# A hybrid decoder step: the sampled tokens' caches go through load, GpSimd product and VectorE sum in three staggered steps, and their HGRN states are loaded one item ahead

## The chip, the cores and the metric

One core of one Trainium2 chip runs the whole program. The metric is the device time of one execution in microseconds, taken as the median of several runs. Five instruction streams matter: PE (TensorE, matmuls), DVE (VectorE), ACT (ScalarE), POOL (GpSimd) and SP (SyncE, which issues every DMA of this kernel). Each stream is worked off in order, and an instruction that waits for a semaphore holds up everything behind it on its own stream.

## The reference

One layer of a decoder trunk, all in float32, for a prompt of 2048 tokens and 8 sampled tokens (one new token for each of 8 sequences with caches). Cut to what matters here:

```python
u = rmsnorm(h) @ w_in                       # 1024 -> 10752 columns, prompt and sampled tokens together
# A: dilated window attention, 3 groups x 8 heads x 64;  B: HGRN2, 4 heads, state 128x128
# C: cross-attention, 4 heads x 128, 256 memory tokens;  then three sigmoid merge gates
# sampled tokens:
s = einsum('bshd,bsjhd->bshj', q, cached_k) * Dh**-0.5       # A: 129 keys, each sequence its own cache
o = einsum('bshj,bsjhd->bshd', softmax(s), cached_v)
S_new = f * S_old + k outer v;  o = S_new^T q                # B: 8 sequences x 4 heads of 128x128
sc = einsum('bthd,bmhd->bhtm', q, mem_k);  oc = einsum('bhtm,bmhd->bthd', softmax(sc), mem_v)   # C
merged = sig(ga) * (ya @ w_pa) + sig(gb) * (yb @ w_pb) + sig(gc) * (yc @ w_pc)
out = h + rmsnorm(merged @ w_out)
```

Every sequence has its own keys and values, so the sampled tokens' products are elementwise work and not matmuls: GpSimd multiplies a block of 128x512 numbers, VectorE sums it.

## The kernel before

The input projection is 36 *units* of 256 columns over five chunks of tokens (512, 384, 384, 384 and 392 wide). Every product is three matmuls (L402, L403, L404), since each operand is split into a rounded part and a rest. The last 24 units are a Python generator, `gate_stream`; beside it run other generators: prompt attention, prompt HGRN, and in the last phase (`phase_rest`) the prompt's cross-attention (`cross`) and `sample`, the sampled tokens' four parts one after the other: `sample_heads`, `sample_attention`, `sample_hgrn`, `sample_cross`. A loop hands out turns: a generator yields (cost, gap), the cost being its matmul time in that step and the gap how long it wants to be left alone before its next turn. While no other generator is due, the next 24 or so matmuls of `gate_stream` are written. So the gaps set only one thing directly: the order of the matmuls on PE, which is kept exactly as written (`manual_schedule(engines={PE})`). On the other engines a scheduler places the instructions when the program is built, by dependences and by its own estimate of times.

After the loop comes the branch stage: matmuls at L163 to L165 (`mm3`), with weights loaded at L1214 and split at L1215 and L1216, inputs loaded at L1226 and split at L1227 and L1229, products with the gates at L1250.

What the change touches:

- Cache blocks. A block of keys or values is 128x512 numbers (256 KB). It lands in one of three slots of the ring `skv`, GpSimd multiplies it in place (L1000 keys, L1027 values, L1094 memory keys, L1121 memory values), VectorE sums it (L1001; L1029 and L1030; L1095; L1123 and L1124). There are 20, 20, 16 and 16 blocks. Between keys and values stands a softmax over all blocks' scores. At the end of each part one small matmul gathers the result (L1036 for the window caches, L1128 for the memory).
- HGRN items. Eight items (4 heads x 2 halves of the batch). Each loads a state of 256 KB into one of two buffers (`ss0`, L1058) and the values, repeated over 128 partitions, into a slot of `skv` (L1061); GpSimd multiplies (L1062), VectorE scales the state and adds (L1063, L1064), the new state is stored (L1065), and after a gap of 2 us four tiny matmuls read it (L1069).
- `cross` writes its score matmuls at L898, its maxima at L899, its normalisation on VectorE at L907, the transposes on PE at L918 that need L907, and the value matmuls at L929. Every gate chunk leaves PSUM through L494 on VectorE. There are three PSUM banks for the gate stream.

Of the kernel before, what the change touches and what calls it, by code (L numbers as in the profile page):

```python
# [10 lines left out]
F32 = mybir.dt.float32  # L11
F32R = mybir.dt.float32r
AF = mybir.ActivationFunctionType
ALU = mybir.AluOpType
# [83 lines left out]
def tile_hybrid_step(ctx: ExitStack, tc: tile.TileContext, I: dict, O: dict):  # L98
# [854 lines left out]
    def sample_heads(sps, pool):  # L953

        cols = pool.tile([128, 28, DEC], F32, tag="scols", name="s_cols", bufs=1)
        dma(cols[:, 0:12, :], qT[:, :, SEQ:NT].rearrange("j p b -> p j b"))
        dma(cols[:, 12:24, :], kT[:, :, SEQ:NT].rearrange("j p b -> p j b"))
        dma(cols[:, 24:28, :], cqT[:, :, SEQ:NT].rearrange("j p b -> p j b"))
        yield 0.0, 5.0
        for i in range(7):  # L960
            ps = sps.tile([128, 512], F32, tag="sp", name="s_pr")
            for j in range(4):
                T.transpose(ps[:DEC, j * 128:j * 128 + 128], cols[:, i * 4 + j, :], ident)
            row = pool.tile([128, 512], F32, tag="skv", name="s_row", bufs=3)[:DEC, :]
# [17 lines left out]

    def sample_attention(sps, pool):
# [5 lines left out]
        for g in range(3):  # L989
# [7 lines left out]
            for j0 in range(0, nj[g], 8):  # L997
                kc = pool.tile([128, 8, 64], F32, tag="skv", name="s_kc", bufs=3)
                dma(kc, I[f"kc{g}"][:, j0:j0 + 8, :])
                G.tensor_tensor(kc, kc, q.unsqueeze(1).to_broadcast([128, 8, 64]), op=ALU.mult)  # L1000
                V.tensor_reduce(sc[:, base[g] + j0:base[g] + j0 + 8], kc, axis=AX.X, op=ALU.add)  # L1001
                yield 0.0, SA_GAP
# [19 lines left out]
        for g in range(3):  # L1022
            for j0 in range(0, nj[g], 8):
                vc = pool.tile([128, 8, 64], F32, tag="skv", name="s_vc", bufs=3)
                dma(vc, I[f"vc{g}"][:, j0:j0 + 8, :])
                pj = sc[:, base[g] + j0:base[g] + j0 + 8]
                G.tensor_tensor(vc, vc, pj.unsqueeze(2).to_broadcast([128, 8, 64]), op=ALU.mult)  # L1027
                t = pool.tile([128, 64], F32, tag="st64", name="s_t", bufs=1)
                V.tensor_reduce(t, vc.rearrange("p j d -> p d j"), axis=AX.X, op=ALU.add)  # L1029
                V.tensor_tensor(o, o, t, op=ALU.add)  # L1030
                yield 0.0, SA_GAP
# [12 lines left out]
    def sample_hgrn(sps, pool):  # L1044
# [8 lines left out]
        for h in range(4):  # L1053
            hgrn_gates(pool, e[:, h, :], lb[:, h:h + 1], oml[:, h:h + 1], f[:, h, :], kin[:, h, :], DEC)
            for b0 in (0, 4):
                bs = slice(b0, b0 + 4)
                s0 = pool.tile([128, 4, 128], F32, tag="ss0", name="s_s0")
                dma(s0, I["state"][:, h, bs, :])  # L1058
                vb = pool.tile([128, 4, 128], F32, tag="skv", name="s_vb", bufs=3)
                sh = [128, 4, 128]  # L1060
                dma(vb, vS[bs, 1536 + h * 128:1664 + h * 128].unsqueeze(0).to_broadcast(sh))  # L1061
                G.tensor_tensor(vb, vb, kin[:, h, bs].unsqueeze(2).to_broadcast(sh), op=ALU.mult)  # L1062
                V.tensor_tensor(s0, s0, f[:, h, bs].unsqueeze(2).to_broadcast(sh), op=ALU.mult)  # L1063
                V.tensor_tensor(s0, s0, vb, op=ALU.add)  # L1064
                dma(O["hg_s"][bs, h].rearrange("b k v -> k b v"), s0)  # L1065
                yield 0.0, SA_GAP
                for b in range(4):
                    c = h * DEC + b0 + b
                    T.matmul(po[:, c:c + 1], lhsT=s0[:, b, :], rhs=q[:, h, b0 + b:b0 + b + 1], start=True, stop=True)  # L1069
                yield 1.65, 0.0  # L1070
# [15 lines left out]
    def sample_cross(sps, pool):  # L1086
# [4 lines left out]
        for j in range(16):  # L1091
            kc = pool.tile([128, 4, 128], F32, tag="skv", name="s_xk", bufs=3)
            dma(kc, I["mkc"][:, j * 4:j * 4 + 4, :])
            G.tensor_tensor(kc, kc, q.unsqueeze(1).to_broadcast([128, 4, 128]), op=ALU.mult)  # L1094
            V.tensor_reduce(s[:, j * 4:j * 4 + 4], kc, axis=AX.X, op=ALU.add)  # L1095
            yield 0.0, SA_GAP
# [21 lines left out]
        for j in range(16):  # L1118
            vc = pool.tile([128, 4, 128], F32, tag="skv", name="s_xv", bufs=3)
            dma(vc, I["mvc"][:, j * 4:j * 4 + 4, :])  # L1120
            G.tensor_tensor(vc, vc, s[:, j * 4:j * 4 + 4].unsqueeze(2).to_broadcast([128, 4, 128]), op=ALU.mult)  # L1121
# [3 lines left out]
            yield 0.0, SA_GAP  # L1125
# [299 lines left out]
```

## Time and profile before

| | |
|---|---|
| median of 3 runs | 3144.35 us (3142.03 to 3147.8) |
| the profiled execution | 3151.64 us, span 3149.9 us |
| PE / LDWEIGHTS / VectorE / ScalarE / GpSimd busy | 96% / 87% / 45% / 32% / 32% |
| first to last small transposes of `sample_heads` (L963) | from 2319.5 us to 2337.8 us |
| matmul after the window caches (L1036) | 2535.3 us |
| HGRN matmuls (L1069) | 2539.7 to 2583.9 us |
| matmul after the memory caches (L1128) | 2675.2 us |

PE is the long engine, so what matters are the places where it stands still. In the rows of the profile, times in brackets are the idle time of the engine just before an instruction and what ended it. A matmul's duration overlaps the next matmul's; the pace is the distance of two starts. PEclk is the share of the TensorE clock that was granted.

### The profile page before, as it was taken

To read this page: it belongs to the slowest core of one execution; us is meant where nothing else is said; L and a number is where in the kernel's file an instruction comes from. 1 tells how busy PE (TensorE), PEld (TensorE's weight loads), DVE (VectorE), ACT (ScalarE), POOL (GpSimd) and SP (SyncE) were. 2 spreads that over 40 slices of the span, in tenths; PEclk is the share of its full clock that TensorE was granted. 3 is DMA by queue.
4 is the path that set the end of the run, shared out by engine and by line. 5 is a ranking of instruction groups with operands and counts; after the bars stand their busy time and mean duration, and the time that the engine had idled before them with its cause. 6 is when DMAs were issued, how large, how long until landed. Compare 5 with 4: busy or idle time off the path is not lost. (4 is left out here: it accounts for less than half of the span.)

```text
span 3149.9 us, 56777 instructions
## 1 busy us (share of the span) xinstructions
PE 3017.3 (96%) x22028; PEld 2746.6 (87%) x22028; DVE 1402.9 (45%) x3635; ACT 995.7 (32%) x2468; POOL 1020.5 (32%) x836
## 2 busy tenths in 40 slices
PE   6999999999999999999899999999998988999998
PEld 6999999999999887878788888888886877899986
DVE  8700002222223555465652376777757356233232
ACT  4412110000003654444551344444443433201222
POOL 4312126556654112020222331121125125634411
PEclk9999999999999999999999999999999999999999
DMA  4333222122213457475645322232246466666442
GB/s 138 102 99 88 72 74 81 61 74 77 71 68 108 120 144 196 136 199 140 175 126 161 98 87 93 88 103 92 90 129 181 116 167 213 199 180 178 155 147 95
DMA packets 369311, 387.54 MB, mean 123 GB/s; under 512 B 87881, under 2 KB 292297, under 8 KB 365713
## 3 DMA queue, kind: packets, MB, share of 16 engines
q1 hardware_dynamic: 369040, 383.91, 41.2%
q8 instruction: 173, 2.83, 0.4%
q14 instruction: 98, 0.79, 0.1%
HBM read 245.13 MB, written 138.67 MB: 122 GB/s over the span
## 5 line engine op out<-in xcount | busy, mean ns | idle before, releaser
L402 PE MATMUL bank<-rnd 128*128 128x384 f32 (+2 forms) x2880 | 1041.4, 362 | 14.7 <-DVE side L494 8.4
L404 PE MATMUL bank<-rnd 128*128 128x384 f32 (+2 forms) x2880 | 1009.1, 350 | 4.6 <-POOL rnd L201 4.6
L403 PE MATMUL bank<-rnd 128*128 128x384 f32 (+2 forms) x2880 | 1009.2, 350 | 0.0
L402 PEld LDWEIGHTS bank<-rnd 128*128 128x128 f32 x2880 | 548.7, 191 | 55.0 <-DVE side L494 9.4
L404 PEld LDWEIGHTS bank<-rnd 128*128 128x128 f32 x2880 | 547.8, 190 | 30.2 <-POOL rnd L201 5.5
L403 PEld LDWEIGHTS bank<-rnd 128*128 128x128 f32 x2880 | 548.8, 191 | 23.1 <-issue 1.9
L163 PE MATMUL bank<-rnd 128*128 128x256 f32 (+4 forms) x1648 | 531.4, 322 | 8.6 <-DVE raw L1250 4.9
L165 PE MATMUL bank<-rnd 128*128 128x256 f32 (+4 forms) x1648 | 528.4, 321 | 4.3 <-POOL rnd L248 4.3
L164 PE MATMUL bank<-rnd 128*128 128x256 f32 (+4 forms) x1648 | 528.7, 321 | 0.6 <-DVE rnd L1229 0.6
L201 POOL TENSOR_TENSOR rnd<-raw,rnd 128x512 fp32r<-128x512 f32 x172 | 227.7, 1331 | 610.7 <-ACT rnd L200 609.3
L163 PEld LDWEIGHTS bank<-rnd 128*128 128x128 f32 (+1 forms) x1648 | 312.6, 190 | 25.1 <-issue 4.2
L165 PEld LDWEIGHTS bank<-rnd 128*128 128x128 f32 (+1 forms) x1648 | 312.6, 190 | 17.8 <-POOL rnd L248 5.3
L164 PEld LDWEIGHTS bank<-rnd 128*128 128x128 f32 (+1 forms) x1648 | 312.7, 190 | 13.8 <-DVE rnd L1229 1.3
L200 ACT CAST rnd<-raw 128x512 fp32r<-128x512 f32 x172 | 106.1, 619 | 631.8 <-PE bank L403 453.8
L450 DVE TENSOR_TENSOR raw<-bank,raw 128x384 f32<-128x384 f32 (+2 forms) x120 | 70.4, 587 | 444.2 <-POOL side L455 214.6
L583 ACT ACTIVATE raw<-raw 128x256 f32<-128x256 f32 (+1 forms) x384 | 172.9, 452 | 152.4 <-DVE raw L581 152.3
L491 POOL TENSOR_TENSOR side<-side 128x384 f32<-128x384 f32 (+2 forms) x60 | 65.6, 1093 | 260.2 <-ACT side L490 242.3
L495 ACT ACTIVATE side<-side 128x384 f32<-128x384 f32 (+2 forms) x120 | 65.5, 546 | 242.7 <-DVE side L494 236.6
L1250 DVE TENSOR_TENSOR raw<-raw,bank 128x412 f32<-128x412 f32 (+1 forms) x120 | 66.9, 579 | 166.4 <-DMA raw<-sgT 87.1
L696 POOL TENSOR_TENSOR side<-side 128x512 f32<-128x512 f32 x32 | 51.1, 1596 | 241.0 <-DMA side<-stC 74.9
L1254 POOL TENSOR_TENSOR raw<-raw 128x412 f32<-128x412 f32 (+1 forms) x80 | 89.8, 1123 | 96.2 <-DVE raw L1250 90.1
L598 ACT COPY raw<-bank 128x256 f32<-128x256 f32 (+1 forms) x192 | 87.2, 492 | 101.1 <-PE bank L596 99.3
(265 smaller groups left out, 3896.5 us busy)
## 6 DMA issues: line engine op xcount, KB each, us to landing
raw<-in_w_t SPq DMA_DIRECT2D x144, 256.0 KB
raw<-sgT SPq DMA_DIRECT2D x96, 206.0 KB
sgT<-side SPq DMA_DIRECT2D x72, 192.0 KB
qT<-side SPq DMA_DIRECT2D x12, 1028.0 KB
out_kT<-side SPq DMA_DIRECT2D x12, 1028.0 KB
out_vN<-raw SPq DMA_DIRECT2D x96, 128.0 KB
raw<-qT SPq DMA_DIRECT2D x96, 128.0 KB
raw<-out_kT SPq DMA_DIRECT2D x96, 128.0 KB
```

Source lines behind the costliest of these rows:

```text
L163: T.matmul(out, lhsT=lh, rhs=rh, start=(i == 0), stop=False)
L164: T.matmul(out, lhsT=lh, rhs=rl, start=False, stop=False)
L165: T.matmul(out, lhsT=ll, rhs=rh, start=False, stop=(i == n - 1))
L200: A.copy(hi, raw)
L201: G.tensor_tensor(lo, raw, hi.bitcast(F32), op=ALU.subtract)
L402: T.matmul(ps[:, :w], lhsT=hi, rhs=xh[c][:, k, :], start=(k == 0), stop=False)
L403: T.matmul(ps[:, :w], lhsT=hi, rhs=xl[c][:, k, :], start=False, stop=False)
L404: T.matmul(ps[:, :w], lhsT=lo, rhs=xh[c][:, k, :], start=False, stop=(k == KT - 1))
L450: V.tensor_tensor(t1[:, :w], ps[:, :w], rc[:, c0:c0 + w], op=ALU.mult)
L583: A.activation(sm[:, :w], sm[:, :w], AF.Exp, scale=-1.0, bias=nmc, accum_out=sts[hp][:, g, 1, h, idx:idx + 1])
L598: A.copy(pts[:, :, :nb, :], pt[:, :, :nb, :])
L1254: G.tensor_tensor(acc[:, :w], acc[:, :w], gt[:, :w], op=ALU.add)
```

## The change

The ring `skv` has four slots in place of three. Key and value blocks of all four passes go through a new generator `in_turn`: in step i block i is loaded, block i-1 is multiplied, block i-2 is summed, and each step yields a gap of 2 us, so each pass has two steps more than it has blocks. In `sample_hgrn` the loads of item i are written ahead of the work on item i-1; the gaps of an item are 2.5 us after the loads and 4.0 us between the new state and its matmuls, where there was 2.0 us.

```diff
+    def in_turn(pool, srcs, first, second):
+        n, tiles = len(srcs), {}
+        for i in range(n + 2):
+            if i < n:
+                tiles[i] = pool.tile([128] + list(srcs[i].shape[1:]), F32, tag="skv", name="s_c", bufs=4)
+                dma(tiles[i], srcs[i])
+            if 0 < i <= n:
+                first(i - 1, tiles[i - 1])
+            if i > 1:
+                second(i - 2, tiles.pop(i - 2))
+            yield 0.0, SA_GAP
...
-            for j0 in range(0, nj[g], 8):
-                kc = pool.tile([128, 8, 64], F32, tag="skv", name="s_kc", bufs=3)
-                dma(kc, I[f"kc{g}"][:, j0:j0 + 8, :])
+            def multiply(i, kc):
                 G.tensor_tensor(kc, kc, q.unsqueeze(1).to_broadcast([128, 8, 64]), op=ALU.mult)
-                V.tensor_reduce(sc[:, base[g] + j0:base[g] + j0 + 8], kc, axis=AX.X, op=ALU.add)
-                yield 0.0, SA_GAP
+            def reduce(i, kc):
+                V.tensor_reduce(sc[:, base[g] + 8 * i:base[g] + 8 * i + 8], kc, axis=AX.X, op=ALU.add)
+            yield from in_turn(pool, [I[f"kc{g}"][:, j0:j0 + 8, :] for j0 in range(0, nj[g], 8)], multiply, reduce)
...
-        for h in range(4):
-            hgrn_gates(...)
-            for b0 in (0, 4):
-                s0 = ...; dma(s0, I["state"][:, h, bs, :])
-                vb = ...; dma(vb, vS[...])
+        for i in range(len(items) + 1):
+            if i < len(items):
+                h, b0 = items[i]
+                s0 = pool.tile(sh, F32, tag="ss0", name="s_s0")
+                dma(s0, I["state"][:, h, b0:b0 + 4, :])
+                vb = pool.tile(sh, F32, tag="skv", name="s_vb", bufs=4)
+                dma(vb, vS[...])
+                states[i] = s0, vb
+                yield 0.0, 2.5
+            if i == 0:
+                continue
+            h, b0 = items[i - 1]
+            s0, vb = states.pop(i - 1)
+            if b0 == 0:
+                hgrn_gates(...)
                 G.tensor_tensor(vb, vb, kin...); V.tensor_tensor(s0, s0, f...); V.tensor_tensor(s0, s0, vb, op=ALU.add)
                 dma(O["hg_s"][bs, h].rearrange("b k v -> k b v"), s0)
-                yield 0.0, SA_GAP
+            yield 0.0, 4.0
                 # 4 matmuls (128x1); yield 1.65, 0.0
```

The window values, the memory keys and the memory values get the same edit as the window keys, with `weigh` and `add` for the values. In the rows below, lines of the changed kernel are: L989 every cache load, L1074 a state's load, L1076 the values' load, L1086 GpSimd's product for an HGRN item, L1089 the state's store, L1093 its matmuls, L1098 the HGRN norm's matmul, L1039 the window values' product, L1116 and L1119 product and sum of memory keys, L1144, L1148 and L1149 those of memory values, L1154 the matmul after the memory caches, L1240 and L1242 load and split of branch weights, L1252 and L1255 those of branch inputs, L1276 the product with the gates (L1250 before).

PE, at the end of the gate stream, before: one matmul of the sampled tokens stands between the last gate matmul (L404) and the branch stage (L163).

```order
L404 MATMUL bank_96<-rnd 128x392
L1128 MATMUL bank_103<-c_sel_c,f_15660 128x32
L163 MATMUL bank_98<-rnd 128x412
L164 MATMUL bank_98<-rnd 128x412
L165 MATMUL bank_98<-rnd 128x412
```

The same place now.

```order
L404 MATMUL bank_96<-rnd 128x392
L1093 MATMUL bank_103<-f_15660 128x1 x4
L1098 MATMUL bank_103<-f_15660,ones_v 128x32
L1154 MATMUL bank_103<-c_sel_c,f_15660 128x32
L163 MATMUL bank_98<-rnd 128x412
```

What moved: the eighth HGRN item's matmuls and the HGRN norm have come down to the end of the gate stream. In all, the first L1069 stood 487 rows ahead of L163 and the eighth 386; the first L1093 stands 277 rows ahead and the eighth 3.

POOL, from the window values to the branch stage, before.

```order
L1027 TENSOR_TENSOR side<-side 128x512 x11
L1062 TENSOR_TENSOR side<-side 128x512 x5
L201 TENSOR_TENSOR rnd<-raw,rnd 128x512 x8
L1062 TENSOR_TENSOR side<-side 128x512 x3
L1094 TENSOR_TENSOR side<-side,f_15660 128x512 x16
L1121 TENSOR_TENSOR side<-side,f_15660 128x512 x3
L201 TENSOR_TENSOR rnd<-raw,rnd 128x512 x2
L1121 TENSOR_TENSOR side<-side,f_15660 128x512 x8
L1229 TENSOR_TENSOR rnd<-raw,rnd 128x824
```

And now (L201 splits the last weights of the gate stream).

```order
L1039 TENSOR_TENSOR side<-side 128x512 x20
L1086 TENSOR_TENSOR side<-side,f_15660 128x512 x6
L201 TENSOR_TENSOR rnd<-raw,rnd 128x512 x10
L1086 TENSOR_TENSOR side<-side,f_15660 128x512
L1255 TENSOR_TENSOR rnd<-raw,rnd 128x824
L1242 TENSOR_TENSOR rnd<-raw,rnd 128x512
L1086 TENSOR_TENSOR side<-side,f_15660 128x512
L1242 TENSOR_TENSOR rnd<-raw,rnd 128x512 x2
L1255 TENSOR_TENSOR rnd<-raw,rnd 128x824
L1116 TENSOR_TENSOR side<-side,f_15660 128x512
L1255 TENSOR_TENSOR rnd<-raw,rnd 128x824
L1116 TENSOR_TENSOR side<-side,f_15660 128x512
```

What moved: 19 of the 32 products of the memory caches stood ahead of the split of the gate stream's last two weight pieces; now none does, and they stand among the branch stage's splits.

SP, around the state loads of the sixth to the eighth item, before (L498 stores one chunk of a gate, so that two of them are a chunk apart).

```order
L1058 DMA f_15660<-in_state 128x512
L498 DMA sgT<-side 128x384
L1065 DMA out_hg_s<-f_15660 128x4x128
L1061 DMA side<-out_vS 128x4x128
L1065 DMA out_hg_s<-f_15660 128x4x128
L931 DMA yT<-raw 128x512
L1058 DMA f_15660<-in_state 128x512
L1093 DMA side<-in_mkc 128x512
L926 DMA raw<-szT 128x512
L1058 DMA f_15660<-in_state 128x512
```

And now, from the seventh state's load; each of these state loads waits on a semaphore of PE.

```order
L1074 DMA f_15660<-in_state 128x512
L498 DMA sgT<-side 128x384
L989 DMA side<-in_mkc 128x512 x2
L1240 DMA raw<-in_w_br 128x4x128 x2
L498 DMA sgT<-side 128x384
L1089 DMA out_hg_s<-f_15660 128x4x128
L989 DMA side<-in_mkc 128x512 x3
L1074 DMA f_15660<-in_state 128x512
```

What moved: behind the eighth state's load 18 chunks of gates were still to be stored, and one memory block stood ahead of it; now four chunks are left behind it, and seven memory blocks stand ahead.

More of the change, by code (lines that the diff above doesn't have):

```diff
@@ L1022, in sample_attention, with weigh, add @@
         for g in range(3):
[L1023 to L1026, printed above, removed]
+            def weigh(i, vc):
+                pj = sc[:, base[g] + 8 * i:base[g] + 8 * i + 8]
                 G.tensor_tensor(vc, vc, pj.unsqueeze(2).to_broadcast([128, 8, 64]), op=ALU.mult)
+            def add(i, vc):
                 t = pool.tile([128, 64], F32, tag="st64", name="s_t", bufs=1)
@@ L1030, in sample_attention @@
                 V.tensor_tensor(o, o, t, op=ALU.add)
-                yield 0.0, SA_GAP
+            yield from in_turn(pool, [I[f"vc{g}"][:, j0:j0 + 8, :] for j0 in range(0, nj[g], 8)], weigh, add)
             e = base[g] + nj[g]
@@ L1052, in sample_hgrn @@
         po, pn = bank[:, 0:32], bank[:, 32:64]
-        for h in range(4):
-            hgrn_gates(pool, e[:, h, :], lb[:, h:h + 1], oml[:, h:h + 1], f[:, h, :], kin[:, h, :], DEC)
-            for b0 in (0, 4):
[L1056 to L1070, printed above, removed]
+        sh = [128, 4, 128]
@@ new lines, in sample_hgrn @@
+        items, states = [(h, b0) for h in range(4) for b0 in (0, 4)], {}
+        for i in range(len(items) + 1):
[4 more added lines that the diff above has]
+                vb = pool.tile(sh, F32, tag="skv", name="s_vb", bufs=4)
+                dma(vb, vS[b0:b0 + 4, 1536 + h * 128:1664 + h * 128].unsqueeze(0).to_broadcast(sh))
+                states[i] = s0, vb
[3 more added lines that the diff above has]
+            h, b0 = items[i - 1]
+            bs = slice(b0, b0 + 4)
+            s0, vb = states.pop(i - 1)
+            if b0 == 0:
+                hgrn_gates(pool, e[:, h, :], lb[:, h:h + 1], oml[:, h:h + 1], f[:, h, :], kin[:, h, :], DEC)
+            G.tensor_tensor(vb, vb, kin[:, h, bs].unsqueeze(2).to_broadcast(sh), op=ALU.mult)
+            V.tensor_tensor(s0, s0, f[:, h, bs].unsqueeze(2).to_broadcast(sh), op=ALU.mult)
+            V.tensor_tensor(s0, s0, vb, op=ALU.add)
+            dma(O["hg_s"][bs, h].rearrange("b k v -> k b v"), s0)
+            yield 0.0, 4.0
+            for b in range(4):
+                c = h * DEC + b0 + b
+                T.matmul(po[:, c:c + 1], lhsT=s0[:, b, :], rhs=q[:, h, b0 + b:b0 + b + 1], start=True, stop=True)
+            yield 1.65, 0.0
@@ L1090, in sample_cross, with multiply, reduce @@
         s = pool.tile([128, 64], F32, tag="sxs", name="s_xs", bufs=1)
-        for j in range(16):
-            kc = pool.tile([128, 4, 128], F32, tag="skv", name="s_xk", bufs=3)
-            dma(kc, I["mkc"][:, j * 4:j * 4 + 4, :])
+        def multiply(i, kc):
             G.tensor_tensor(kc, kc, q.unsqueeze(1).to_broadcast([128, 4, 128]), op=ALU.mult)
-            V.tensor_reduce(s[:, j * 4:j * 4 + 4], kc, axis=AX.X, op=ALU.add)
-            yield 0.0, SA_GAP
+        def reduce(i, kc):
+            V.tensor_reduce(s[:, 4 * i:4 * i + 4], kc, axis=AX.X, op=ALU.add)
+        yield from in_turn(pool, [I["mkc"][:, j * 4:j * 4 + 4, :] for j in range(16)], multiply, reduce)
         m = pool.tile([128, 4], F32, tag="sxm", name="s_xm", bufs=1)
@@ L1117, in sample_cross, with weigh, add @@
         V.memset(o, 0.0)
[L1118 to L1121, printed above, removed]
+        def weigh(i, vc):
+            G.tensor_tensor(vc, vc, s[:, 4 * i:4 * i + 4].unsqueeze(2).to_broadcast([128, 4, 128]), op=ALU.mult)
+        def add(i, vc):
             t = pool.tile([128, 128], F32, tag="sxt", name="s_xt", bufs=1)
@@ L1124, in sample_cross @@
             V.tensor_tensor(o, o, t, op=ALU.add)
-            yield 0.0, SA_GAP
+        yield from in_turn(pool, [I["mvc"][:, j * 4:j * 4 + 4, :] for j in range(16)], weigh, add)
         yield 0.0, SA_LAG
```

2 lines of the change are left out of this document (1 added, 1 removed).

## The prediction, made before the changed kernel ran

> **What bounds the kernel now.** I read the page first, then the busy times by stretch, the PE timeline where it stands still, and the timelines of the engines that it waits for.
>
> ```profile
> span 3149.9 us, 56777 instructions
> PE 3017.3 (96%) x22028; PEld 2746.6 (87%) x22028; DVE 1402.9 (45%) x3635; ACT 995.7 (32%) x2468; POOL 1020.5 (32%) x836
> ```
>
> PE is busy for all but 133 us. A change that touches no matmul can win only where PE stands still and lose only where it makes PE stand. The table by stretch says where the sampled tokens' work costs anything (columns: stretch, its length, busy us of PE, its weight loads, VectorE, ScalarE, GpSimd, granted clock, DMA share, GB/s).
>
> ```profile
> 2319.60:2535.30 215.70, 191.57 (x966) 167.19 (x963) 121.38 (x279) 90.88 (x231) 68.59 (x61) 0.95 0.53 146
> 2390.00:2430.00 40.00, 32.41 (x158) 27.69 (x157) 37.49 (x80) 16.67 (x46) 22.01 (x24) 0.96 0.68 203
> 2450.00:2535.00 85.00, 85.00 (x437) 74.91 (x436) 31.20 (x80) 41.53 (x104) 12.10 (x10) 0.99 0.41 116
> 2535.30:2675.00 139.70, 118.35 (x610) 107.30 (x610) 82.00 (x162) 50.86 (x111) 60.39 (x48) 0.95 0.70 201
> 2675.00:2745.00 70.00, 62.72 (x323) 60.99 (x322) 18.81 (x31) 19.19 (x31) 46.04 (x36) 0.98 0.63 186
> ```
>
> From the first small transposes to the matmul behind the window caches PE idles 24.1 us, from there to the end of the gate stream (2675 us) 21.4 us, at the start of the branch stage 7.3 us. The stretch 2450 to 2535, where only prompt work and gates run, has none. So at most 53 us of idle time are to be had, and the slow clock behind each stop:
>
> ```profile
> 2373.78 1.08 PE L918 MATMUL bank<-ident,raw 128*128 128x128 f32 x4 [3.84 <-DVE raw L907]
> 2447.55 1.11 PE L918 MATMUL bank<-ident,raw 128*128 128x128 f32 x4 [10.72 <-DVE raw L907]
> 2564.70 1.11 PE L918 MATMUL bank<-ident,raw 128*128 128x128 f32 x4 [5.59 <-DVE raw L907]
> 2643.66 0.45 PE L402 MATMUL bank<-rnd 128*128 128x384 f32 x1 [2.37 <-DVE side L494]
> 2647.78 0.34 PE L404 MATMUL bank<-rnd 128*128 128x384 f32 x1
> 2652.36 0.44 PE L402 MATMUL bank<-rnd 128*128 128x384 f32 x1 [4.24 <-DVE side L494]
> 2655.37 0.52 PE L403 MATMUL bank<-rnd 128*128 128x384 f32 x1
> 2655.69 0.52 PE L404 MATMUL bank<-rnd 128*128 128x384 f32 x1
> ```
>
> The 24 matmuls of a chunk take 4.1 us from the first start (2643.66) to the last (2647.78), 0.18 us each. After the stop of 4.24 us the starts are 0.32 us apart for about 3 us, which loses some 1.5 us. With two to four such stops in each of the first two stretches I put them at 29 us each, idle and slow clock together.
>
> Who holds PE up is the cross-attention's normalisation (L907) or a gate's evacuation (L494) on VectorE, and these stand in VectorE's queue behind sums that wait for GpSimd, which waits for a load:
>
> ```profile
> 2431.53 0.23 DVE L1030 TENSOR_TENSOR side<-side 128x64 f32<-128x64 f32 x1
> 2437.95 0.69 DVE L1064 TENSOR_TENSOR f<-f,side 128x512 f32<-128x512 f32 x1 [6.19 <-POOL side L1062]
> 2445.09 0.69 DVE L1064 TENSOR_TENSOR f<-f,side 128x512 f32<-128x512 f32 x1 [5.65 <-POOL side L1062]
> 2429.73 14.14 DMA side<-out_vS
> ```
>
> The last row is from the chain of waits: one load of an HGRN item's values took 14.14 us.
>
> No load, product, sum or store is added or removed in any part; all of the change is order and a slot more.
>
> **Part 1: the window caches.** The edit writes the sum two steps behind the load, but only PE keeps the written order, and on VectorE the sums stand among the same gate evacuations as before, about four to a chunk. What really changes there is the fourth slot. In the key pass a slot's cycle sets the pace:
>
> ```profile
> L1000 POOL TENSOR_TENSOR side<-side x20: 1273/1295/1311, 2339.3 to 2384.5; 128x512 f32<-128x512 f32 x20
> 2339.30:2387.00 47.70, 41.88 (x196) 35.74 (x195) 30.84 (x58) 19.42 (x47) 30.30 (x24) 0.93 0.62 187
> ```
>
> 19 steps in 45.2 us are 2.38 us a block, 7.1 us a slot. Four slots give 1.8 us, 34 us for the pass, above the 1.3 us that GpSimd needs. PE idles 5.8 us in the pass (47.7 less 41.9), some 8 with the slow clock; that should mostly go, I take 7. In the value pass VectorE is busy 37.5 of 40 us (stretch 2390 to 2430), so a slot more brings nothing there: 0. For the two waits behind L1064, the values' loads still come one behind the other (the waits of 6.19 and 5.65 us are for consecutive ones) and are issued one block earlier: 2 of the 10.7 us go. Together 9 us gained; bounds -3 (four such loads in flight together slow the first) and 20.
>
> **Part 2: from there to the gates' end.** The tiny matmuls' gaps add up to 52 us (8 x 6.5) where they were 16, and the passes have 16 steps more (two for each of eight runs of blocks). On PE the first L1093 now stands 277 rows ahead of L163, at about 0.2 us a row 55 us, and the last one behind the gates. So between the window caches and that point PE sees only what the clean stretch 2450 to 2535 shows. Then come the HGRN items, one each 8 us of matmuls. The load of item i waits until PE has read item i-2, 16 us ahead of its own matmuls. A load takes
>
> ```profile
> 2551.05 11.62 DMA f<-in_state
> 2569.44 6.63 DMA f<-in_state
> ```
>
> so with 1.4 us on VectorE (0.69 each above) it is in time for items 3 to 7. The wait for PE is one on SP: behind each state's load stand a gate chunk's store, memory blocks and branch weights. Three banks and two output buffers give a gate chunk about two chunks, 8 us, before PE feels a late store, so I cost this at nothing; if loads took 16 us, PE would stop at each item. The memory sums, which made VectorE late at 2643 and 2652, have left this stretch nearly all. What stays are the branch inputs' splits on VectorE. I take 22 of the 29 us as gained; bounds 10 and 29.
>
> **Part 3: the memory caches, behind the gates.** Here the change costs. Before, the last memory sum was done 17 us ahead of the gates' end, and the matmul behind it cost nothing:
>
> ```profile
> L1128 PE MATMUL bank<-c_sel_c,f x2: 190/232/273, 2675.2 to 2675.2; 128*128 128x32 f32 x2
> 2658.03 0.59 DVE L1124 TENSOR_TENSOR f<-f 128x128 f32<-128x128 f32 x1
> ```
>
> Now L1154 still stands ahead of every branch matmul, and the memory blocks must take the slots of HGRN values that are freed only by the sums of items 5 to 8. PE then waits with nothing else to do. I follow the slot of item 8, with 0 at the end of the gate matmuls.
>
> - Item 8's state waits for PE's item 6, some 63 gate matmuls x 0.18 = 11 us ahead of 0, and stands on SP behind memory blocks whose slots are not yet free: issued at -7. With 6.6 us of loading and 1.4 of VectorE, the slot is free at +1 (-5 to +6).
> - Memory keys 4, 8, 12 and 16 pass through this slot one after the other. Pace before:
>
> ```profile
> L1094 POOL TENSOR_TENSOR side<-side,f x16: 1262/1291/1415, 2576.7 to 2610.1; 128x512 f32<-128x512 f32 x16
> 2618.46 3.04 POOL L1121 TENSOR_TENSOR side<-side,f 128x512 f32<-128x512 f32 x3 [7.04 <-DVE f L1115]
> L1121 POOL TENSOR_TENSOR side<-side,f x16: 1037/1042/1812, 2618.5 to 2654.7; 128x512 f32<-128x512 f32 x16
> L1123 DVE TENSOR_REDUCE f<-side x16: 1028/1080/1123, 2619.5 to 2656.6; 128x128 f32<-128x512 f32 x16
> L1124 DVE TENSOR_TENSOR f<-f x16: 276/407/1758, 2621.0 to 2658.0; 128x128 f32<-128x128 f32 x16
> L1216 POOL TENSOR_TENSOR rnd<-raw,rnd 128x512 fp32r<-128x512 f32 x24 | 31.6, 1327 | 28.3 <-ACT rnd L1215 22.2 <-DMA raw<-in_w_br 6.2
> ```
>
> 15 steps in 33.4 us, 2.23 us a block, 6.7 us a slot's cycle: 4 x 6.7 = 27, to +28 (22 to 32 for the term).
> - The softmax between the passes left GpSimd 7.0 us without work: +35 (6 to 7).
> - 16 value blocks took 15 steps of 2.41 us; a slot's cycle of 7.2 us over four slots is 1.8 us, 29 us (24 to 38). GpSimd's own work in it is no less than 16 x 1.04 and, by POOL's order, about seven branch-weight splits of 1.3: 26 us. With 2 us for the last sums: L1154 at +66.
>
> The VectorE addition L1124 took from 0.28 to 1.76 us for the same shape. The Trainium skill, page "SBUF — State Buffer", section "SBUF: two separate sides", says that VectorE and GpSimd hold one pair of ports exclusively for a whole instruction when VectorE reads two SBUF tensors. The spread here looks like that, though these rows alone don't prove it. By that rule the additions and GpSimd's products exclude each other, 16 x (1.04 + 0.28) + 7 x 1.3 = 30 us in place of 29, and the tail would be 67 us; it speaks against a gain from the fourth slot in this pass.
>
> **Part 4: the branch stage.** Its weights and first inputs are split while PE waits, so the 7.3 us at its start go; the slow clock after the long stop costs 2, and I keep 1 for a late load: 4 us gained (0 to 7).
>
> **Sum.** +66 - 9 - 22 - 4 = +31 us. On the profiled execution (3151.64 us) this gives 3183; that execution lies 7.3 us above the median, and both sides of the comparison are medians, so 3144.35 + 31 = 3175 us.
>
> **The rivals.**
>
> *A: faster.* The tail shrinks below what the other parts give back. The place is the fourth slot. If item 8's state lands 5 us ahead of 0, slot cycles take 5.5 us since the gates' stores are gone, and the values run at GpSimd's 26 us less the splits, the tail is -5 + 22 + 6 + 24 = 47 us; against it parts 1, 2 and 4 at their upper bounds, 20 + 29 + 7 = 56: -9 us, 3135. It decides at a tail equal to the gains, 35 us at my values. Against it: no shorter tail comes out of any row, and the gains would have to be whole. 0.06; and 0.06 for landing within 0.2% (6 us) of before, about what a measurement of this kernel can tell from no change.
>
> *B: the staging does nothing.* VectorE's order hardly changes, so its waits stay: part 1 gives 0, part 2 only 17, since branch splits and late states hold the evacuations. +66 - 0 - 17 - 4 = +45, 3189. For it: the scheduler's order. Against it: the 2.38 us pace is a slot's. 0.2.
>
> *C: SP is the brake.* SP works in order, and memory blocks, weight and input loads of the branch stage and gate stores stand there mixed; each waits for its own slot. If 29 of the 32 blocks are still to come at 0, since the freed slots take only the first three until then, and go at the 2.75 us a block of before's whole memory part (32 blocks between 2569.9, the first load's issue, and 2658), the tail is 80 + 7 = 87 us: +52, 3196; with B's gains 3210. 0.13.
>
> ```profile
> L1093 SPq DMA_DIRECT2D side<-in_mkc x16: 327/333/614, 2569.9 to 2607.2; - x16
> ```
>
> **How the numbers follow.** My forecast, slower by 15 to 42 us, has 0.55; B 0.2 and C 0.13 are slower as well; A's two cases 0.12. Slower 0.88, same 0.06, faster 0.06. The range from 3150 to 3204 leaves out A with the same-case and the upper part of C. The likeliest case alone spans 3159 to 3186.
>
> **What would show it.** After: one idle stretch of PE of 50 to 85 us ahead of the first L163, ended by the last memory sum (L1149); L1093's last matmul at the gates' end; the first L1144 about 30 us ahead of that idle stretch's end; the wait of 10.7 us ahead of L918 still there at 8 or so; the key pass of the window caches at about 1.8 us a block; no waits of PE at the start of the branch stage. The prediction is wrong if L1154 runs within 40 us of the last gate matmul, or if PE still loses 20 us or more in the HGRN items.

## Result and profile after

| | before | after |
|---|---|---|
| median of 5 runs | 3147.8 us (3142.03 to 3149.66) | 3195.8 us (3194.89 to 3199.08) |
| span of the profiled execution | 3149.9 us | 3196.2 us |
| first to last small transposes (L963) | from 2319.5 us | from 2314.9 us |
| last gate matmul (L404) | 2675.0 us | 2662.4 us |
| first branch matmul (L163) | 2677.3 us | 2730.1 us |

The five runs of before include the three that the forecast started from.

The change makes the kernel slower: ratio 1.0157, 95% interval 1.0146 to 1.0168, or +48 us where +31 was forecast. The measured 3195.8 us lies inside the stated range of 3150 to 3204, but 10 us above the span of the likeliest case (3159 to 3186). The page of the changed kernel begins:

```profile
span 3196.2 us, 56774 instructions
PE 3012.0 (94%) x22028; PEld 2741.3 (86%) x22028; DVE 1410.5 (44%) x3635; ACT 994.4 (31%) x2468; POOL 1019.1 (32%) x836
```

Every engine is busy as long as before, within 8 us (PE 5 us less); what has grown is PE's idle time. The PE timeline of the changed kernel: starts that waited long, and the first branch matmul (in brackets the wait and what ended it; rows in between are left out):

```profile
2406.99 1.02 PE L918 MATMUL bank<-ident,raw 128*128 128x128 f32 x4 [3.31 <-DVE raw L907]
...
2431.15 1.09 PE L918 MATMUL bank<-ident,raw 128*128 128x128 f32 x4 [8.09 <-DVE raw L907]
2454.14 1.08 PE L918 MATMUL bank<-ident,raw 128*128 128x128 f32 x4 [7.24 <-DVE raw L907]
2467.04 3.78 PE L929 MATMUL bank<-raw 128*128 128x512 f32 x4 [5.66 <-ACT raw L919]
2635.72 0.69 PE L402 MATMUL bank<-rnd 128*128 128x384 f32 x1 [5.67 <-DVE side L494]
2665.54 1.05 PE L1093 MATMUL bank<-f 128*128 128x1 f32 x8 [2.84 <-DVE f L1088]
2671.33 0.64 PE L1098 MATMUL bank<-f,ones_v 128*128 128x32 f32 x2 [4.73 <-ACT f L1096]
2729.67 0.64 PE L1154 MATMUL bank<-c_sel_c,f 128*128 128x32 f32 x2 [57.71 <-DVE f L1149]
2730.12 0.69 PE L163 MATMUL bank<-rnd 128*128 128x412 f32 x1
```

Two things stand out. PE waits 57.7 us for the last memory sum, inside the 50 to 85 us that were forecast. And at the end of the window caches stand three waits of 21 us together, where before there was one of 10.7 us; these were not forecast. The busy times by stretch (columns as in the prediction), first of the kernel before, then of the changed one; the stretches are the window caches and what directly follows them, the rest of the gate stream in two parts, and in the changed kernel the tail:

```profile
2319.50:2459.50 140.00, 115.87 (x581) 101.70 (x580) 92.31 (x206) 51.82 (x133) 59.57 (x54) 0.93 0.61 165
2459.50:2539.50 80.00, 80.00 (x406) 69.04 (x406) 31.67 (x80) 41.79 (x106) 10.32 (x8) 1.00 0.39 117
2539.50:2675.00 135.50, 114.15 (x591) 103.83 (x590) 79.50 (x155) 48.12 (x103) 59.09 (x47) 0.95 0.71 201
```

```profile
2314.90:2474.90 160.00, 127.67 (x612) 110.59 (x611) 96.79 (x216) 56.79 (x149) 60.41 (x56) 0.89 0.57 154
2474.90:2594.90 120.00, 120.00 (x618) 105.29 (x618) 44.09 (x111) 58.45 (x145) 10.28 (x8) 1.00 0.34 106
2594.90:2662.40 67.50, 60.98 (x338) 57.34 (x336) 23.61 (x30) 24.57 (x43) 30.05 (x21) 0.95 0.67 201
2662.40:2730.10 67.70, 2.42 (x14) 1.90 (x13) 49.24 (x88) 15.43 (x30) 48.26 (x41) 0.53 0.67 201
```

PE idles 24.1 us in the window stretch before and 32.3 after; in the rest of the gate stream 21.4 before and 6.5 after; and in the tail 65.3 us, where before it was about 2.

Idle time leaves out the slow clock. So the lost time of a stretch, here and below, is its length less its matmuls at their full pace (0.23, 0.17 and 0.18 us for the gate matmuls of 512, 384 and 392 columns, 0.21, 0.09 and 0.43 for L898, L918 and L929). That gives 32.7 us in the window stretch before and 45.9 after, and 31.3 and 11.1 us for the rest. This is the ledger of the two profiled spans:

| part | forecast | measured |
|---|---|---|
| ahead of the first L963 | 0 | -4.6 |
| 1, window caches | -9 | +13.2 |
| 2, rest of the gate stream | -22 | -20.2 |
| 3, last gate matmul to first branch matmul | +66 | +65.5 |
| 4, branch stage (472.6 to 466.1 us) | -4 | -6.5 |
| remainder: matmul work that left these stretches | - | -1.0 |
| sum | +31 | +46.4 (spans: +46.3) |

The 4.6 us ahead of the first L963 need not be the change's: over all kernels of this study that matmul starts between 2312.3 and 2319.5 us.

The window stretch is what the forecast had wrong. GpSimd and VectorE of the changed kernel, there (parts of their timelines):

```profile
2428.97 1.04 POOL L1086 TENSOR_TENSOR side<-side,f 128x512 f32<-128x512 f32 x1 [6.37 <-DMA side<-out_vS]
2436.13 1.04 POOL L1086 TENSOR_TENSOR side<-side,f 128x512 f32<-128x512 f32 x1 [6.12 <-DMA side<-out_vS]
2442.97 1.04 POOL L1086 TENSOR_TENSOR side<-side,f 128x512 f32<-128x512 f32 x1 [5.80 <-DMA side<-out_vS]
2448.86 1.04 POOL L1086 TENSOR_TENSOR side<-side,f 128x512 f32<-128x512 f32 x1 [4.85 <-DMA side<-out_vS]
2457.19 1.04 POOL L1086 TENSOR_TENSOR side<-side,f 128x512 f32<-128x512 f32 x1 [7.29 <-DMA side<-out_vS]
2464.11 1.04 POOL L1086 TENSOR_TENSOR side<-side,f 128x512 f32<-128x512 f32 x1 [5.89 <-DMA side<-out_vS]
```

```profile
2430.04 0.69 DVE L1088 TENSOR_TENSOR f<-f,side 128x512 f32<-128x512 f32 x1 [4.10 <-POOL side L1086]
2450.86 0.69 DVE L930 TENSOR_TENSOR raw<-bank,raw 128x512 f32<-128x512 f32 x1 [10.05 <-DMA raw<-szT]
2464.85 0.56 DVE L494 TENSOR_SCALAR side<-bank 128x384 f32<-128x384 f32 x1 [10.60 <-DMA sgT<-side]
```

Six loads of HGRN values land one by one, 6 to 8 us apart. VectorE first waits for the values themselves (L1088), then for a cross-attention load (`szT`) and for a gate store (`sgT`) that were issued among them; PE waits each time for VectorE, the third time through ScalarE (L919). Before, five such loads stood there; the products of the first three started 7 to 8 us apart, those of the last two 4.1 and 1.6 us behind the one ahead.

### The profile page after: what moved, and what is told of

It is laid out like the page before. It is cut to its first block, busy times and chain, and to the rows that moved or that the text cites. A ratio compares the mean times of both kernels' runs of the same rounds, so it can differ in the third digit from the quotient of the medians.

```text
span 3196.2 us, 56774 instructions
## 1 busy us (share of the span) xinstructions
PE 3012.0 (94%) x22028; PEld 2741.3 (86%) x22028; DVE 1410.5 (44%) x3635; ACT 994.4 (31%) x2468; POOL 1019.1 (32%) x836
## 5 line engine op out<-in xcount | busy, mean ns | idle before, releaser
L404 PE MATMUL bank<-rnd 128*128 128x384 f32 (+2 forms) x2880 | 1006.2, 349 | 3.9 <-POOL rnd L201 3.9
L404 PEld LDWEIGHTS bank<-rnd 128*128 128x128 f32 x2880 | 545.7, 189 | 29.2 <-POOL rnd L201 4.8
L163 PE MATMUL bank<-rnd 128*128 128x256 f32 (+4 forms) x1648 | 531.6, 323 | 1.5 <-ACT rnd L247 1.4
L201 POOL TENSOR_TENSOR rnd<-raw,rnd 128x512 fp32r<-128x512 f32 x172 | 228.6, 1337 | 670.6 <-ACT rnd L200 606.8
L163 PEld LDWEIGHTS bank<-rnd 128*128 128x128 f32 (+1 forms) x1648 | 312.8, 190 | 16.7 <-ACT rnd L247 1.6
L1276 DVE TENSOR_TENSOR raw<-raw,bank 128x412 f32<-128x412 f32 (+1 forms) x120 | 68.3, 581 | 168.6 <-PE bank L165 112.5
L596 PE MATMUL bank<-ident,raw 128*128 128x128 f32 x600 | 99.0, 291 | 21.4 <-ACT raw L583 19.0
```

The lines of the kernel that those rows point to most:

```text
L163: T.matmul(out, lhsT=lh, rhs=rh, start=(i == 0), stop=False)
L201: G.tensor_tensor(lo, raw, hi.bitcast(F32), op=ALU.subtract)
L404: T.matmul(ps[:, :w], lhsT=lo, rhs=xh[c][:, k, :], start=False, stop=(k == KT - 1))
L596: T.transpose(pt[:, h, j, :], sms[h][:, j * 128:j * 128 + 128], ident)
```

## Experiments

Ratios are to the kernel before, run beside each on the same chip. Lines of code differ a little from kernel to kernel.

**Which edit makes the tail?** First the changed kernel with the HGRN loop of before.

```diff
-        for i in range(len(items) + 1):   # loads one item ahead, gaps 2.5 and 4.0
+        for h in range(4):                # as before; ring skv with bufs=4
```

> The changed kernel with the HGRN loop of before (loads, work and matmuls of an item together, gap 2 us) in the ring of four; in_turn stays. On PE the eighth item now stands 37 us of matmul work ahead of the end of the gate matmuls (72 us in the kernel before, behind them in the changed one). Theory, the place of the eighth item sets the tail, since the memory blocks run some 66 us behind it: the wait ahead of the memory matmul is 25 to 35 us in place of 57.7, the time 3160 us (3150 to 3170). Rival, in_turn's two more steps a pass alone make the tail: 57 us again, 3190 us or more. Rival, the HGRN edit alone makes it: no tail, 3148 us or less.

Then the kernel before with the HGRN edit alone.

```diff
-        for h in range(4):                # as before
+        for i in range(len(items) + 1):   # loads one item ahead, gaps 2.5 and 4.0; skv with bufs=3
```

> The kernel before with the HGRN edit alone (loads one item ahead, gaps 2.5 and 4 us), three slots and no in_turn. The eighth item stands 30 us of matmul work ahead of the gates' end. Theory, the place of the eighth item sets the tail: a wait of 30 to 40 us ahead of the memory matmul, 3168 us (3158 to 3180). Rival, the edit alone makes the whole tail: 57 us, 3195 us. Rival, in_turn makes it: no wait, 3148 us. In the window stretch three slots let at most three loads of values lie in the DMA queue: if the burst of such loads is what costs the changed kernel 14 us there, the stretch loses no more here than before (32 us).

And the changed kernel with short gaps.

```diff
-                yield 0.0, 2.5
+                yield 0.0, 0.0
...
-            yield 0.0, 4.0
+            yield 0.0, 2.0
```

> The changed kernel with the gaps of an HGRN item cut from 2.5 and 4.0 us to 0 and 2.0 us, all else kept: loads one item ahead, in_turn, four slots. The eighth item stands 37 us of matmul work ahead of the gates' end. Theory, its place sets the tail: the wait ahead of the memory matmul is 25 to 35 us, the time 3162 us (3150 to 3172). Rival, SyncE's queue or GpSimd's splits of branch weights set the tail whatever the place of the items: 50 to 58 us again, 3190 us. The three waits of 8.1, 7.2 and 5.7 us at the end of the window caches stay, since the loads are the same.

Measured: 3184.3 us (1.0104, 1.0089 to 1.0119) for the old HGRN loop, 3162.7 us (1.0035, 1.0021 to 1.0048) for the HGRN edit alone, 3175.5 us (1.008, 1.0064 to 1.0095) for the short gaps. The wait for the memory matmul on PE in each of the three, in this order:

```profile
2702.15 0.63 PE L1145 MATMUL bank<-c_sel_c,f 128*128 128x32 f32 x2 [19.43 <-DVE f L1140]
```

```profile
2695.28 0.64 PE L1137 MATMUL bank<-c_sel_c,f 128*128 128x32 f32 x2 [33.65 <-DVE f L1133]
```

```profile
2703.32 0.64 PE L1154 MATMUL bank<-c_sel_c,f 128*128 128x32 f32 x2 [23.60 <-DVE f L1149]
```

So the place of the eighth item sets the tail, as the theory had it, though two of the waits (19.4 and 23.6 us) are shorter than the 25 to 35 us expected. Both edits feed it: in_turn by its extra steps, the HGRN edit by its gaps, each because it moves the eighth item's matmuls towards the gates' end. What stays nearly constant is the distance from those matmuls to the memory matmul: 64 us in the changed kernel (2665.5 to 2729.7), 68 with the old loop (2634.3 to 2702.2), 73 with the HGRN edit alone (2622.0 to 2695.3), 68 with short gaps (2634.9 to 2703.3). Before, the eighth item ran at 2583.2 and the last memory sum at 2658.0, 75 us later and still ahead of the gates' end. With the HGRN edit alone and three slots PE idles 23.7 us in the window stretch (2319.2 to 2459.2), against 24.1 before: by itself this edit brings no loss there.

The times of the first and third came out 24 and 13 us above what was expected, in part since items close behind each other wait for their own sums. With the old loop PE waited 12.5 us for one item's sum, with short gaps 9.5 us; the longer gaps of the change do hide that, and pay for it in the tail.

**Is it the values' load?** The changed kernel with a plain block in its place.

```diff
-                dma(vb, vS[b0:b0 + 4, 1536 + h * 128:1664 + h * 128].unsqueeze(0).to_broadcast(sh))
+                dma(vb, I["state"][:, h, b0:b0 + 4, :])
```

> The changed kernel with the values of an HGRN item loaded as a plain 256 KB block (the state's, 2 KB a partition) in place of a row repeated over 128 partitions in pieces of 512 bytes; so the new states and what is read from them are other numbers, with the same instructions. Theory, the repeated loads of 7 us each, six in one burst, hold gate stores and cross-attention loads up behind them in the DMA queue, and through VectorE PE: the waits of 8.1, 7.2 and 5.7 us go to less than 3 us each, 3178 us (3172 to 3184), with the tail at 55 us or so as it was. Rival, the waits come from where the sums stand in VectorE's queue or from the four slots: they stay, 3196 us.

Measured: 3165.4 us (1.0046, 1.0029 to 1.0063), 30 us less than the changed kernel (33 us when each is set against the kernel before that ran beside it), and 13 us less than expected. The three waits became one of 3.84 us, and the tail stayed (54.4 us). The lost time in the window stretch fell from 45.9 to 24.8 us, that in the rest of the gate stream from 11.1 to 2.4. The wait of 5.67 us at 2635.72 is gone too, which the expectation had left out. So these eight loads cost the changed kernel some 30 us.

**Is it the fourth slot or the staging?** The kernel before with four slots and nothing else.

```diff
-... tag="skv", ... bufs=3
+... tag="skv", ... bufs=4
```

> The kernel before with a fourth slot in the ring skv and nothing else: no in_turn, HGRN loop as before. On PE the order is that of before. Theory, the fourth slot alone brings the loss in the window stretch (one load of values more in a row in the DMA queue): from the first small transposes to some 155 us on PE loses 46 us as in the changed kernel, not 33 as before, with two waits of 6 to 8 us, 3164 us (3157 to 3170). Rival, the staged order of in_turn brings it: 33 us there and 3150 us. A third way, the fourth slot shortens the key pass as I forecast: 26 us there, 3143 us.

Measured: 3165.4 us (1.0055, 1.004 to 1.007), as the first theory had it: the slot alone brings the loss. The lost time in the window stretch is 49.0 us, and the same three waits stand there, with in_turn absent:

```profile
2436.15 1.09 PE L918 MATMUL bank<-ident,raw 128*128 128x128 f32 x4 [8.56 <-DVE raw L907]
...
2458.57 1.08 PE L918 MATMUL bank<-ident,raw 128*128 128x128 f32 x4 [6.71 <-DVE raw L907]
...
2470.62 2.93 PE L929 MATMUL bank<-raw 128*128 128x512 f32 x3 [4.66 <-ACT raw L919]
```

The three steps of the change can now be added up, each kernel against the kernel before that ran beside it: four slots +16 us, in_turn on top (the old-loop kernel) +18, the HGRN edit on top of both +14, each uncertain by some 5 us.

The slot is not useless everywhere. With it alone the products of the memory values start within 26.6 us, where the kernel before took 36.2 (2618.5 to 2654.7):

```profile
L1121 POOL TENSOR_TENSOR side<-side,f x16: 1035/1042/1147, 2627.2 to 2653.8; 128x512 f32<-128x512 f32 x16
```

That pass ends ahead of the gates' end in both kernels, so PE gains nothing from it there.

**Is it the queue or what the load does to the DMA engines?** The changed kernel with these loads issued by ScalarE.

```diff
-                dma(vb, vS[...])
+                A.dma_start(vb, vS[...])
```

> The changed kernel with the loads of the HGRN items' values issued by ScalarE in place of SyncE, so that they lie in a queue of their own. Theory, what comes behind such a load waits because it is behind it in the same queue: the 10 us for an activation's load and for a gate store go, and with them the second and third wait of PE (7.2 and 5.7 us); the first (8.1 us, VectorE itself waits for the values) stays: 3183 us (3176 to 3188). Rival, the DMA engines that work on the repeated row are what is busy, whichever queue asks: all three waits stay, 3196 us, or more where ScalarE itself stands behind a slot.

Measured: 3193.9 us (1.0147, 1.0132 to 1.0163); no gain that can be told from none. The profile lists these loads in a queue of their own (2.10 MB). VectorE's wait for the gate store shrank from 10.6 to 3.0 us, but the one for the activation grew to 11.8, and one of PE's waits to 10.3. SyncE issued that activation's load (`szT`) at 2437.3 us and VectorE went on with it at 2452.9: what is under way beside such loads waits, also in another queue. It is not a clean test, since ScalarE itself stood up to 5.4 us behind one of these loads, whose slot was not yet free. The Trainium skill, page "DMA: Bandwidth & Descriptors", section "Issuing engines are not separate DMA queues", says that transfers from all issuers run on the same DMA engines; the wait of 11.8 us agrees.

**What makes the load slow?** HGRN items of one sequence and four heads, first in the changed kernel, then in the kernel before. The diff is cut: the gates of all four heads are now computed ahead of the loop, and the new states are stored by sequence.

```diff
-    a["state"] = f["state_hgrn"][0].transpose(2, 1, 0, 3)
+    a["state"] = f["state_hgrn"][0].transpose(2, 0, 1, 3)
...
-                dma(vb, vS[b0:b0 + 4, 1536 + h * 128:1664 + h * 128].unsqueeze(0).to_broadcast(sh))
+                dma(vb.rearrange("p h v -> p (h v)"), vS[i, 1536:2048].unsqueeze(0).to_broadcast([128, 512]))
```

> The changed kernel with HGRN items of one sequence and all four heads in place of one head and four sequences, and the state input laid out to match: the values are then one run of 2 KB repeated over 128 partitions, no longer four of 512 bytes; the state is 2 KB a partition as before. Work and gaps are the same. Theory, the pieces of 512 bytes make the load slow: a load takes 2 to 3 us, the three waits at the end of the window caches go as with the plain block, 3166 us (3160 to 3175) with a tail of 55 us. Rival, that all 128 partitions read one row is what makes it slow: 7 us again, 3196 us.

> The kernel before with the same items of one sequence and four heads, three slots, no in_turn, loads not ahead. Theory of the 512-byte pieces: the wait of 10.7 us at the end of the window caches goes, and of the late states and evacuations in the HGRN stretch some 8 us with it: 3132 us (3125 to 3140). Rival, the repeated row is slow in any piece: 3150 us.

And the changed kernel with 512 pieces of 512 bytes, none read twice.

```diff
-                dma(vb, vS[b0:b0 + 4, 1536 + h * 128:1664 + h * 128].unsqueeze(0).to_broadcast(sh))
+                dma(vb, I["state"][:, :, (2 * h + b0 // 4) % DEC, :])
```

> The changed kernel with the values of an HGRN item loaded from the state input in 512 pieces of 512 bytes, each from another place, in place of four rows of 512 bytes repeated over 128 partitions; so the new states are other numbers, with the same instructions. Theory, pieces of 512 bytes alone make such a load take 7 us: the three waits at the end of the window caches (8.1, 7.2 and 5.7 us) stay and the time is 3195 us. Rival, it takes both, small pieces and one row read 128 times: the load takes 2 to 3 us, the waits go as with the plain block, 3166 us (3160 to 3175).

Measured: 3168.0 us (1.0062, 1.0047 to 1.0077) for the changed kernel by sequence; 3132.9 us (0.9949, 0.9933 to 0.9966) for the kernel before by sequence, the fastest of all; 3171.8 us (1.0049, 1.0032 to 1.0065) for the pieces. The first two came out as the theory of the 512-byte pieces had it, but the third refutes that pieces of 512 bytes are enough: its rival, that it takes both, held. The plain block and the pieces differ from the changed kernel in the load alone. In the kernel before by sequence GpSimd gets its values 2 to 3 us apart, and PE's wait of 10.7 us is one of 2.85:

```profile
2432.84 1.05 POOL L1061 TENSOR_TENSOR side<-side 128x512 f32<-128x512 f32 x1 [2.00 <-DMA side<-out_vS]
2436.04 1.05 POOL L1061 TENSOR_TENSOR side<-side 128x512 f32<-128x512 f32 x1 [2.15 <-DMA side<-out_vS]
2438.34 1.05 POOL L1061 TENSOR_TENSOR side<-side 128x512 f32<-128x512 f32 x1 [1.25 <-DMA side<-out_vS]
```

One row repeated over 128 partitions is fast when its run is 2 KB, and 512 pieces of 512 bytes are fast when each is read once. Of the forms tried, only four rows of 512 bytes, each read 128 times, are slow. The busy times by stretch (the last two columns are the busy share of the DMA engines and GB/s) while such loads are under way, of the changed kernel:

```profile
2422.00:2428.00 6.00, 1.05 (x5) 0.56 (x3) 3.95 (x9) 2.50 (x7) 0.60 (x1) 0.96 0.15 39
2429.00:2435.00 6.00, 3.85 (x13) 3.36 (x14) 1.35 (x4) 0.58 (x1) 1.01 (x1) 0.55 0.51 74
2436.00:2442.00 6.00, 6.00 (x31) 4.89 (x30) 3.04 (x8) 3.00 (x8) 1.04 (x1) 1.00 0.63 62
2449.00:2455.00 6.00, 0.86 (x5) 0.90 (x5) 2.71 (x7) 2.48 (x7) 0.90 (x1) 0.71 0.32 68
```

of the one by sequence:

```profile
2425.00:2433.00 8.00, 2.42 (x11) 1.90 (x10) 8.00 (x16) 2.87 (x8) 4.44 (x5) 0.83 0.77 205
```

and of the one with single pieces:

```profile
2426.00:2434.00 8.00, 4.20 (x16) 3.29 (x15) 7.96 (x17) 3.09 (x8) 4.73 (x5) 0.73 0.80 249
```

In these four stretches of the slow form all DMA engines together move 39 to 74 GB/s, even with other transfers beside it (busy share up to 0.63); the fast forms run at 205 and 249 in the stretches shown. These are chosen stretches: over 2422 to 2464 us the three kernels move 86, 157 and 160 GB/s. In the first row hardly anything but the slow load is under way, and the busy share is 0.15, by which some 2.4 of 16 engines would be busy (an estimate, 0.15 x 16). So the transfer itself does not fill the engines. Why just this pattern is slow, none of the runs tells.

**Is the fourth slot harmful by itself, and does the change work without its two faults?** Three more with items by sequence. The kernel before with four slots:

```diff
+        for b in range(DEC):   # items by sequence
-... tag="skv", ... bufs=3
+... tag="skv", ... bufs=4
```

> The kernel before with HGRN items by sequence (values in runs of 2 KB) and a fourth slot in the ring, no in_turn, no look-ahead. Theory, the fourth slot did harm only because one more slow load of values lay in a row with the others: with fast ones it costs nothing, 3133 us (3127 to 3140). Rival, the fourth slot itself changes VectorE's or SyncE's order for the worse: 15 us more than with three, 3148 us.

the kernel before with a smaller gap:

```diff
+        for b in range(DEC):   # items by sequence, three slots
-SA_GAP = 2.0
+SA_GAP = 1.0
```

> The kernel before with HGRN items by sequence and the gap of a step (SA_GAP) cut from 2 to 1 us. The eighth item then stands 124 us of matmul work ahead of the gates' end and the memory matmul 47 us ahead of it, 77 us behind the eighth item. Theory, the memory matmul needs 60 to 75 us behind the eighth item, so it makes PE wait little, and the last 47 us of gates and the branch stage's start lose nothing: 3126 us (3118 to 3135). Rival, the same waits only come earlier: 3133 us. Rival, the memory matmul stands too early and PE waits for it: over 3140 us.

and the changed kernel with smaller gaps:

```diff
+        for i in range(DEC + 1):   # items by sequence, loads one item ahead; gaps 0.0 and 2.0
-SA_GAP = 2.0
+SA_GAP = 1.6
```

> The changed kernel (in_turn, loads one item ahead, four slots) with HGRN items by sequence, gaps of an item 0 and 2 us, and SA_GAP 1.6 us. The eighth item stands 86 us of matmul work ahead of the gates' end. Theory, the memory matmul comes 60 to 75 us behind the eighth item, so there is no tail, and the slow loads are gone: 3132 us (3122 to 3142), as the kernel before with fast loads. Rival, the staging brings a tail of its own wherever the items stand: a wait over 15 us, 3150 us or more.

Measured: 3137.8 us (0.9958, 0.9941 to 0.9974), 3139.7 us (0.9969, 0.9956 to 0.9982) and 3134.8 us (0.9952, 0.9937 to 0.9967). With fast loads the fourth slot no longer costs 16 us; what may be left, 3137.8 against 3132.9, is not told apart by these intervals. So its theory held, and so did that of the staged kernel: with the eighth item far enough ahead it has no tail:

```profile
2658.66 0.30 PE L1152 MATMUL bank<-c_sel_c,f 128*128 128x32 f32 x2
2659.26 0.46 PE L163 MATMUL bank<-rnd 128*128 128x412 f32 x1 [0.30 <-DVE side L494]
```

Yet it is no faster than the kernel before by sequence. The smaller gap missed its forecast of 3126 us by 14 us: the memory matmul made PE wait for nothing and the last 47 us of gates ran clean, but the waits only came earlier, among them 6.7 us at 2556.6 and 3.8 us at an HGRN item. The lost time up to the last gate matmul is 47.3 us in the kernel before by sequence, 56.2 with the smaller gap, 51.6 in the staged one.

## Why the prediction was right and wrong

**Part 3, the tail: right, nearly step by step.** Item 8's slot was to be free 1 us behind the gates' end (-5 to +6); its last sum (L1088) ended 3.1 us behind it. The steps behind it, products and sums of the memory caches in the changed kernel:

```profile
L1116 POOL TENSOR_TENSOR side<-side,f x16: 1256/1275/2045, 2639.0 to 2689.9; 128x512 f32<-128x512 f32 x16
```

```profile
L1144 POOL TENSOR_TENSOR side<-side,f x16: 1031/1039/1089, 2697.6 to 2725.1; 128x512 f32<-128x512 f32 x16
```

```profile
L1149 DVE TENSOR_TENSOR f<-f x16: 291/808/1155, 2699.8 to 2729.3; 128x128 f32<-128x128 f32 x16
```

With 0 at 2662.4, the last key product starts at +27.5 (forecast: keys done at +28), the first value product at +35.2 (+35), L1154 at +67.3 (+66). The value blocks run at 1.83 us (27.5 us for 15 steps; forecast 1.8). For the values the fourth slot did what the sum said (26.6 us against 36.2 with the slot alone). That the average of a stop-and-go row hit so well for the keys is partly luck: they came in bursts between branch-weight splits. The term that the value pass took, first product to L1154, was 32.1 us against my 31. The sum by the rule of the Trainium skill, page "SBUF — State Buffer", section "SBUF: two separate sides", was one microsecond higher, too little to decide between the two. The median addition L1149 took 0.81 us, where L1124 took 0.41 before, in a stretch where GpSimd is busy 26.5 of 32.5 us (2697.6 to 2730.1), which agrees with that rule without proving it.

**Part 2: right, 20 us gained for 22.** About half of what was left is the 5.67 us wait at 2635.72, which is gone where the values' loads are fast. There one step failed: a state's load was not in time. VectorE waited 10.4 us for it (L1087, to 2632.6), and the gate's evacuation behind it held PE up:

```profile
2632.61 0.92 DVE L1087 TENSOR_TENSOR f<-f 128x512 f32<-128x512 f32 x1 [10.39 <-DMA f<-in_state]
```

**Part 4: right in sign, 6.5 us for 4.** PE has next to no waits there. After the stop its starts were 0.34 us apart for 4.6 us (2730.12 to 2734.73), then 0.19: 14 matmuls lost 2.2 us, where 2 were forecast.

**Part 1: wrong, and this is the whole miss** (-9 forecast, +13 measured; a difference of 22, against 17 in the total). Two steps failed.

The first: "19 steps in 45.2 us are 2.38 us a block, 7.1 us a slot", so that a fourth slot would give 1.8. It gave nothing in this pass: 19 steps in 45.9 us in the changed kernel, 48.7 with the slot alone. The mean hid two different things, as GpSimd's timeline of the changed kernel shows (parts of it):

```profile
2345.44 1.30 POOL L1011 TENSOR_TENSOR side<-side 128x512 f32<-128x512 f32 x1 [0.92 <-DMA side<-in_kc]
2351.94 7.82 POOL L1011 TENSOR_TENSOR side<-side 128x512 f32<-128x512 f32 x6 [5.20 <-DMA side<-in_kc]
2361.22 2.54 POOL L1011 TENSOR_TENSOR side<-side 128x512 f32<-128x512 f32 x2 [1.46 <-DMA side<-in_kc]
2368.07 1.28 POOL L201 TENSOR_TENSOR rnd<-raw,rnd 128x512 fp32r<-128x512 f32 x1 [4.31 <-ACT rnd L200]
2371.01 1.41 POOL L201 TENSOR_TENSOR rnd<-raw,rnd 128x512 fp32r<-128x512 f32 x1 [1.67 <-PE bank L403]
```

Six products run in 7.82 us, 1.30 each, at GpSimd's own pace; between stand stops that no slot shortens. One (5.20 us) is at the change of the group, where SyncE first waits for the old group's last product to load new queries and holds the next keys up behind them. Another is where weight splits (L201) stand ahead of the keys and wait for ScalarE and PE. The kernel before has the same stop, of 5.05 us, at its first change of group:

```profile
2359.62 3.83 POOL L1000 TENSOR_TENSOR side<-side 128x512 f32<-128x512 f32 x3 [5.05 <-DMA side<-in_kc]
```

The second: for the two waits behind L1064, "2 of the 10.7 us go". I had seen that one load of values took 14.14 us and that they came one behind the other, and named "four such loads in flight together" as a bound of 3 us lost. The price of the fourth slot is 16 us, as the kernel with that slot alone shows, and it goes when the loads are fast. By the timelines it is one load more in the burst, with an activation's load and a gate store caught between; that detail is read, not tested by itself.

**The rivals.** B (+45) and C (+52) both named a total nearer to +48 than my +31, but not the reason. In B part 1 gives nothing and part 2 a little less: part 1 did not stay, it got worse by the slow loads, and part 2 gained all but 2 us. C's tail of 87 us and A's gain did not come. That +48 lies in the stated range owes something to its width: an unforeseen loss of 13 us in part 1, in place of a gain of 9, still fitted. Of the signs I had set, the stretch of 50 to 85 us ended by L1149, L1093 at the gates' end, the first L1144 32 us ahead of that stretch's end, and the quiet branch start were seen; the key pass at 1.8 us a block and the wait falling from 10.7 to 8 were not: there are three waits now, the longest 8.1.

## What to carry to other kernels

Before a mean pace is read as a buffer's cycle, look at the timeline behind it: if work runs in bursts at the engine's own pace, with stops between, more buffers buy nothing there, and they may let one more slow transfer into a burst. Where the slots do set the pace, as in the memory values, one more helped (36.2 to 26.6 us). Work that a later stage must wait for is measured by its distance to that stage: here the last memory sum starts 60 to 68 us behind the last HGRN item's matmuls in every kernel with four slots, and 73 to 76 us in every one with three, so every gap ahead of that item that brings it within this distance of the gates' end becomes idle time of PE. A load that takes three times as long as others of its size deserves a look at its access pattern before any reordering: items by sequence gained 16 us, the reordering lost 48.

## What the runs showed of the hardware

Loads of 256 KB that read four rows of 512 bytes 128 times each landed 6 to 8 us apart in the changed kernel. In either of two close forms, one row of 2 KB read 128 times or 512 different pieces of 512 bytes, they landed some 2 to 3 us apart. With the slow form under way all DMA traffic of the core together ran at 39 to 74 GB/s in four stretches of 6 us, and with hardly anything beside it the DMA engines were busy for a share of 0.15. Issuing it from another engine, in a queue of its own, did not free the transfers beside it: VectorE still waited 11.8 us for one.
